# A two-layer decoder trunk: first projections by pairs of row blocks, cond fetched first, ada groups placed behind the compression, elementwise work moved from POOL to DVE and ACT

## The chip, the cores and the metric

The kernel runs on one core of a Trainium2 chip. The metric is the device time of one execution in microseconds (us). An execution that the hardware profiler recorded is read here by its engines: PE (matrix products and transposes), DVE (vector), ACT (activations), POOL (the second elementwise engine) and SP, whose queue issues nearly all weight loads.

## The reference

The reference is a trunk of two layers over 256 tokens of width 1024, all in float32. Each layer is a mixer and a mixture of experts, both behind a norm that is scaled and shifted by a vector made of the condition `c` ("ada"):

```python
cond = jax.nn.silu(c)
for layer in range(DEPTH):                      # DEPTH = 2
    mod = cond @ ada_w[layer] + ada_b[layer]    # 1024 x 6144
    sh1, sc1, g1, sh2, sc2, g2 = jnp.split(mod, 6, axis=-1)
    h = modulate(rms_norm(x, norm_mix[layer]), sh1, sc1)
    y = nsa_conv_mixer(h, ...) if layer % 2 == 0 else rwkv_pool_mixer(h, ...)
    x = x + g1[:, None, :] * y
    h = modulate(rms_norm(x, norm_ffn[layer]), sh2, sc2)
    x = x + g2[:, None, :] * grouped_moe(h, ...)   # 16 experts, top 2 of one group
return rms_norm(x, final_norm)
```

The mixer of layer 0 is sparse attention beside a gated convolution. Its attention has three branches: keys and values compressed by a small MLP with GELU, blocks selected by the compressed scores, and a window. The mixer of layer 1 is RWKV-7 (a recurrence over time with decay, here solved in chunks) beside causal means over windows of 2 to 16 tokens.

## The kernel before

Tokens lie in two blocks of 128 (`tt`), channels in eight row blocks of 128 (`kt` or `ct`). Weights come as pieces of 1 MB (128 x 2048 float32). `stream` takes the next slot of a ring of `NB` = 10 buffers and issues the load on SP's queue, so a load starts only when the last reader of its slot is through, and SP's queue is served in order. Engines run their instructions in the order that the program's scheduler fixed at build time. `tc.issue_after(d)` is a bound for that scheduler: what is inside comes behind the instruction `d`.

The work runs in stages, by the profiled execution: start and projections (0 to 61 us), compression (61 to 91), the attention loop (91 to 171), router and gather of layer 0 (`into_moe`, 171 to 207), its experts (`moe`, 207 to 413), the transition (413 to 429), the mixer of layer 1 (`mixer1`, 429 to about 587), its router (587 to 617), its experts (617 to 823) and the tail.

The ada vectors aren't made on PE. Weight pieces are laid out with the output on the partitions, and each piece takes two DVE instructions at L200 (`scalar_tensor_tensor` with a running sum, 128 x 1024), four for a group `ada(l, n)` of 512 outputs. Each layer has twelve groups, 48 of these instructions. Groups 0 to 3 are wanted by the first norm, 4 and 5 by the residual gate, 6 to 11 by the norm and gate of the experts. In layer 0, groups 0 to 3 stand in front of the projections (`TokProj`, L456 to L471, PE L471), 4 and 5 behind them, 6 and 7 in the compression, 8 behind it, and the list `more` in the attention loop (L720 to L735, ten steps `i`) names the others and three groups of layer 1. The fourth, (1, 3), is loaded in `moe` and computed in `start` (L1609).

The compression takes the GELU at L611 to L616 (tile `hg`), PE L625 and L630, the scores at L644 to L658 (`Pc`), and the transposes L664. `fill.run(n)` puts n units of the convolution's projections (PE L557, two row blocks each) into PE's order at such places, so that PE has work while DVE and ACT finish a chain. `heat(n)` issues n matrix products whose result nobody reads.

In layer 1, weights are split into a high part (ACT, L387) and a rest (L388, POOL or DVE by the list `engs` of `Parts`); a projection is three products per row block (PE L426). Behind it stands one long chain through DVE, ACT and POOL: shifts (L1198), key norms and gates (L1233 to L1271, POOL at L1246 and L1255), `AR` (POOL L1277), `rk` (DVE L1282), the chunk products (PE L1322, masks on DVE L1324 and L1326 and on POOL L1330 and L1332), `solve` (L1340, a triangular inverse of small DVE steps from PE L1345 on), `spread`, and the levels (PE L1374, DVE L1380 and L1386) that fold the chunks. The windowed means are `pooled` (POOL L1426, then PE L1440).

In the router, `choose` (L769) turns logits into a selection (L783 to L799), `place` (PE L808) into positions. `split` (L292) makes the high part and the rest of the normed tokens, the rest on ACT and POOL (L299, L300).

## Time and profile before

| | us |
|---|---|
| median of 3 executions | 836.95 (835.94 to 837.11) |
| the profiled execution's own time | 836.91 |
| its span, first to last instruction | 835.2 |
| PE busy in the span | 745.1 (89%) |
| DVE busy | 441.8 (53%) |
| ACT busy | 222.9 (27%) |
| POOL busy | 103.2 (12%) |
| moved by DMA | 291.34 MB, 349 GB/s in the mean |

A share of the whole span says little here, since the stages have different limits: the two expert stages, half of the span, keep PE busy nearly without a gap, and POOL does nothing in them. So the views are read stage by stage: the busy time of each engine in a stretch, what PE waited for, and which instructions of an engine are long where another runs beside them.

### The profile page before, as it was taken

To read this page: it belongs to the slowest core of one execution; us is meant where nothing else is said; L and a number is where in the kernel's file an instruction comes from. 1 tells how busy PE (TensorE), PEld (TensorE's weight loads), DVE (VectorE), ACT (ScalarE), POOL (GpSimd) and SP (SyncE) were. 2 spreads that over 40 slices of the span, in tenths; PEclk is the share of its full clock that TensorE was granted. 3 is DMA by queue.
4 is the path that set the end of the run, shared out by engine and by line. 5 is a ranking of instruction groups with operands and counts; after the bars stand their busy time and mean duration, and the time that the engine had idled before them with its cause. 6 is when DMAs were issued, how large, how long until landed. Compare 5 with 4: busy or idle time off the path is not lost.

```text
span 835.2 us, 12029 instructions
## 1 busy us (share of the span) xinstructions
PE 745.1 (89%) x4778; PEld 419.5 (50%) x4779; DVE 441.8 (53%) x937; ACT 222.9 (27%) x442; POOL 103.2 (12%) x87
## 2 busy tenths in 40 slices
PE   0998989996999999999669859799889999999993
PEld 0556766455353353533268859567553534435331
DVE  5666769954123342223788898986531421434225
ACT  3031313245111121201357633303531201202112
POOL 0000132511000000000223794100110000000000
PEclk9999989998999999999969988899979999999998
DMA  9999959897899999999856175787839999999991
GB/s 362 415 420 421 365 197 344 299 419 297 363 421 422 422 421 421 423 421 424 351 201 252 51 305 226 320 320 287 350 151 421 423 423 421 423 420 423 420 417 73
DMA packets 42689, 291.34 MB, mean 349 GB/s; under 512 B 4864, under 2 KB 5504, under 8 KB 8448
## 3 DMA queue, kind: packets, MB, share of 16 engines
q1 hardware_dynamic: 41760, 288.07, 85.1%
q10 hardware_dynamic: 864, 2.40, 0.8%
q8 instruction: 42, 0.69, 0.3%
q14 instruction: 23, 0.19, 0.1%
HBM read 289.40 MB, written 1.05 MB: 348 GB/s over the span
## 4 chain that ended last, share of the span: by engine, by line
PE 36%; DVE 7%; issue 3%; POOL 2%; ACT 2%; POOLq 0%; DVEq 0%; ACTq 0%
PE ps L985 13%; PE ps L1017 6%; PE ps L426 3%; PE ps L361 3%; PE ps L1374 3%; PE ps L1037 2%; PE ps L900 1%; DVE w L200 1%; DVE slab L1326 1%; POOL wr L388 1%; POOL AR L1277 1%; PE ps L1322 1%; POOL slab L1255 1%; PE ps L773 1%; DVE slab L140 0%
## 5 line engine op out<-in xcount | busy, mean ns | idle before, releaser
L985 PE MATMUL ps<-w,XT 128*64 128x512 f32 x1024 | 223.8, 595 | 0.0
L985 PEld LDWEIGHTS ps<-w,XT 128*64 128x64 f32 x1024 | 73.7, 138 | 146.3 <-issue 143.2
L200 DVE SCALAR_TENSOR_TENSOR w<-w,cond 128x1024 f32<-128x1024 f32 x96 | 120.0, 1279 | 11.5 <-ACT cond L148 6.3
L990 DVE TENSOR_TENSOR sg<-sg,ps 128x512 f32<-128x512 f32 x16 | 11.0, 687 | 199.5 <-PE ps L985 199.5
L1017 PE MATMUL ps<-w,HT 128*64 128x512 f32 x512 | 113.8, 596 | 1.3 <-ACT HT L1004 1.3
L1017 PEld LDWEIGHTS ps<-w,HT 128*64 128x64 f32 x512 | 35.2, 137 | 70.5 <-issue 63.0
L426 PE MATMUL ps<-hT,wr 128*128 128x256 f32 x288 | 56.5, 299 | 5.6 <-issue 4.1
L361 PE MATMUL ps<-w,slab 128*128 128x512 f32 x128 | 61.5, 619 | 0.0
L1022 DVE SCALAR_TENSOR_TENSOR Y<-ps,gw,Y 128x512 fp32r<-128x512 f32 x32 | 24.0, 750 | 63.0 <-ACT Y L1021 63.0
L388 POOL TENSOR_TENSOR wr<-w,wr 128x2048 fp32r<-128x2048 f32 x5 | 24.7, 4943 | 224.0 <-SPq L1079 211.5
L426 PEld LDWEIGHTS ps<-hT,wr 128*128 128x128 f32 x288 | 48.1, 205 | 6.7 <-issue 4.7
L1021 ACT ACTIVATE Y<-ps,gw 128x512 fp32r<-128x512 f32 x32 | 22.0, 687 | 98.2 <-PE ps L1017 98.2
L372 DVE TENSOR_TENSOR x<-x,ps 128x512 f32<-128x512 f32 x72 | 46.3, 679 | 0.3
L557 PE MATMUL ps<-hT,w 128*128 128x256 f32 x192 | 46.0, 397 | 0.0
L371 DVE TENSOR_TENSOR ps<-ps,gb 128x512 f32<-128x512 f32 x64 | 41.4, 692 | 2.6 <-PE ps L1037 2.4
L426 PE MATMUL ps<-lo,wr 128*128 128x256 f32 x144 | 42.5, 295 | 0.0
L1037 PE MATMUL ps<-Y,CT 128*128 128x512 f32 x128 | 39.1, 422 | 2.9 <-ACT Y L1021 1.7
L557 PEld LDWEIGHTS ps<-hT,w 128*128 128x128 f32 x192 | 37.2, 198 | 6.1 <-issue 0.8
L471 PE MATMUL ps<-w,hT 128*128 128x512 f32 (+1 forms) x96 | 36.6, 541 | 0.3 <-ACT hT L271 0.2
L989 ACT ACTIVATE sg<-ps 128x512 f32<-128x512 f32 x16 | 9.6, 597 | 99.2 <-PE ps L985 99.2
L361 PEld LDWEIGHTS ps<-w,slab 128*128 128x128 f32 x128 | 23.4, 195 | 23.4 <-issue 22.2
L271 ACT ACTIVATE XT<-ps,AB 128x256 f32<-128x256 f32 x32 | 18.1, 565 | 62.0 <-PE ps L900 50.8
(319 smaller groups left out, 945.3 us busy)
## 6 DMA issues: line engine op xcount, KB each, us to landing
w<-in_moe_g_dram SPq DMA_DIRECT2D x64, 1024.0 KB, 16.0
w<-in_moe_u_dram SPq DMA_DIRECT2D x64, 1024.0 KB, 14.9
w<-in_moe_d_dram SPq DMA_DIRECT2D x60, 1024.0 KB, 16.0
w<-in_ada_w_dram SPq DMA_DIRECT2D x48, 1024.0 KB, 10.0
w<-in_w_dram SPq DMA_DIRECT2D x19, 1024.0 KB, 11.8
w<-in_wout_dram SPq DMA_DIRECT2D x8, 1024.0 KB, 9.6
w<-in_cmp_w_dram SPq DMA_DIRECT2D x4, 1024.0 KB, 12.9
w<-in_moe_d_dram SPq DMA_DIRECT2D x4, 512.0 KB, 17.9
```

Source lines behind the costliest of these rows:

```text
L200: V.scalar_tensor_tensor(ws, ws, 1.0, cond, op0=OP.mult, op1=OP.mult, accum_out=modc[:, l, k:k + 1])
L361: mm(st[h], self.oT(kt)[:, tt * 128:(tt + 1) * 128], self.ws[h][kt // 4][:, (kt % 4) * 512:(kt % 4 + 1) * 512], start=kt == 4, stop=kt == 3)
L371: V.tensor_mul(po, po, gb[:, sl])
L372: V.tensor_add(x[:, tt, sl], x[:, tt, sl], po)
L388: eng.tensor_tensor(lo, raw, hi, op=OP.subtract)
L426: mm(pq, a, b, start=first and kt == kts[0] and i == 0, stop=last and kt == kts[-1] and i == 2)
L471: mm(self.pq[tt], hT[:, kt, tt * 128:(tt + 1) * 128], self.w[:, k * n:(k + 1) * n], start=kt == 0, stop=kt == 7)
L557: mm(st["pq"], w(kt, ct * 128, ct * 128 + 128), hT[:, kt, :], start=kt == 0, stop=kt == 7)
L985: mm(pg[64 * e:64 * e + 64, :], XT[:, kt, 64 * e:64 * e + 64], ws[kt // 4, e][:, (kt % 4) * 512:(kt % 4 + 1) * 512], start=kt == 0, stop=k ...
L1017: mm(py[64 * e:64 * e + 64, :], HT[:, c, 64 * e:64 * e + 64], ws[e][:, c * 512:(c + 1) * 512], start=c == 0, stop=c == 3)
L1037: mm(po, CT[:, tt], Y[:, i, h * 512:(h + 1) * 512], start=i == 0, stop=i == 1)
L1374: mm(t[x[o], p], left(p, *x), right(p, *x), start=start and p == 0, stop=stop and p == 3)
```

## The change

Nothing that is computed changes. The parts:

- **Ring.** `NB` is 12 for 10, with less scratch for DMA descriptors; in `moe` one buffer of the pool `wq` goes, and 20 pieces of the experts are loaded ahead instead of 19.
- **Start.** `cond` is the first load, in two halves on two queues; its SiLU stands behind the loads of the constants. The first projections go by pairs of row blocks (`pair`, `mod_pair`, `cols`): the ada pieces of one pair, then its products. The bias adds of the first four groups go to DVE.
- **Compression.** `ada(0, 4)` comes behind the last instruction of the GELU, 5 and 6 behind `vcm`, 7 behind `Pc`; `more` holds 8, 9, 10 and 11. Five fills of PE become seven, three become five.
- **Attention loop.** POOL's half of L690 goes to ACT.
- **Router.** The rest in `split` is one DVE instruction (128 x 1024) ahead of the scores; `heat(10)` in layer 0, `heat(4)` for `heat(2)` and the gather ahead of the gate units in layer 1. `ada(1, 3)` moves to the end of layer 0's router.
- **Transition.** The first piece of layer 1's projection is loaded and split inside the last expert step; the rest of it, `heat(16)` and `heat(4)` stand by the norm; both `ab` come first.
- **Mixer of layer 1.** All POOL work goes to DVE: the splits, L1246, L1255, L1277, masks L1330 and L1332, `pooled`. `rk` and the masks come behind `solve`, as do all ada pieces of groups 4 to 11. Copies of `tok_kb` and `tok_v` (half of them DVE L140) go to ACT. `spread` may come at 11 us of filling instead of 14.
- **Tail.** `x * fin` of one half is made early, and ACT scales it; the output is issued ahead of the branch for the overflow.

```diff
-NB = 10
+NB = 12
...
-    nc.scalar.dma_start(cond, bass.AP(tensor=ca.tensor, offset=ca.offset, ap=[[0, 128], [1, D]]))
-    P.activation(cond, cond, AF.Silu)
+    for eng, o in ((nc.sync, 0), (nc.scalar, 64)):
+        eng.dma_start(cond[o:o + 64], bass.AP(tensor=ca.tensor, offset=ca.offset, ap=[[0, 64], [1, D]]))
...
-                G.tensor_tensor(hl[:, 1, sl], t, hl[:, 0, sl], op=OP.subtract)
+            V.scalar_tensor_tensor(hl[:, 1], x[:, tt], r, hl[:, 0], op0=OP.mult, op1=OP.subtract)
...
+        nxt = norm.pair(0)
         for h in range(2):
-            ada(0, h)
-            ada(0, 2 + h)
-            norm.ab(h)
...
+            for q in (2 * h, 2 * h + 1):
+                for n in (h, 2 + h):
+                    cols(n, q % 2, 1 if q else 2)
+                norm.mod_pair(q, nxt)
+                for t in projs[:2]:
+                    if q % 2 == 0:
+                        t.load(h)
+                    t.run(q)
...
-        for n in (4, 5):
-            ada(0, n)
...
-        ada(0, 6)
+        with tc.issue_after(d.ins):
+            ada(0, 4)
         fill.add(chan_units(1304 + 1024, done_cg))
-        fill.run(5)
+        fill.run(7)
...
-        ada(0, 7)
+        with tc.issue_after(d.ins):
+            ada(0, 5)
+            ada(0, 6)
...
-        ada(0, 8)
-        fill.run(3)
+        with tc.issue_after(d.ins):
+            ada(0, 7)
+        fill.run(5)
...
-                    eng = V if hh else G
-                    eng.tensor_scalar(Pt[:, hh, b], Pt[:, hh, b], mx[:, 2 * hh + b, 2:3], None, op0=OP.mult)
+                    if hh:
+                        V.tensor_scalar(Pt[:, hh, b], Pt[:, hh, b], mx[:, 2 * hh + b, 2:3], None, op0=OP.mult)
+                    else:
+                        P.activation(Pt[:, hh, b], Pt[:, hh, b], AF.Copy, scale=mx[:, 2 * hh + b, 2:3])
...
-        more = [(0, 9), (0, 10), (0, 11), None, None, None, None, (1, 0), (1, 1), (1, 2)]
+        more = [(0, 8), (0, 9), (0, 10), None, (0, 11), None, None, (1, 0), (1, 1), (1, 2)]
...
+            heat(10)
             route.place(1)
+            ada(1, 3)
...
+                            gs_.append(Parts(1536, 256, ((None, None),), (V,)).split(lo=False))
+                            first.extend((gs_[0].last, gs_[0].finish(0)))
...
-        gs_.append(Parts(0, 512, (("B6", None), (None, None)), (G, V)))
+        gs_.append(Parts(0, 512, (("B6", None), (None, None)), (V, V)))
...
-        G.tensor_tensor(av, av, kk, op=OP.mult)
+        V.tensor_tensor(av, av, kk, op=OP.mult)
...
-                G.tensor_tensor(SC[c][own, h, :, 0], SC[c][own, h, :, 0], K("scmask")[own, None, 0:64].to_broadcast([64, 4, 64]), op=OP.mult)
...
+        late = deque([weigh] + [lambda c=c: masks(c) for c in range(4)])
...
-                for _ in range(4):
-                    todo.popleft()(last)
+                solved.append(last)
...
-            if steps == 1 and spent >= 14:
+            if steps == 1 and spent >= 11:
...
-        norm.ab(0)
-        for tt in range(2):
-            d = norm.transposes(tt, 0)
-        for h, t in enumerate(todo):
-            with tc.issue_after(d[1] if h else last):
-                ada(1, 3, [t], h)
-        norm.ab(1)
+        for h in range(2):
+            norm.ab(h)
...
-    nc = _bacc.Bacc("TRN2", target_bir_lowering=False, num_devices=1)
+    nc = _bacc.Bacc("TRN2", target_bir_lowering=False, num_devices=1, dynamic_dma_scratch_size=64)
```

The scheduler's order shows where this lands. First DVE's order at the end of the compression, where `m` is the softmax's denominators of the two token blocks, `slab` from `s` is `Pc`, and the instruction on `w, modc` is an ada instruction (L200 before, L201 after). Before:

```order
L655 TENSOR_TENSOR m_546<-m_546,gs 128x8
L655 TENSOR_TENSOR m_568<-m_568,gs 128x8
L657 TENSOR_SCALAR m_546<-m_546,c_m_169 128x8
L658 TENSOR_TENSOR slab_102<-s_567,m_568 128x8x16
L200 SCALAR_TENSOR_TENSOR w,modc<-w,cond 128x1024 x2
L658 TENSOR_TENSOR slab_102<-s_545,m_546 128x8x16
L200 SCALAR_TENSOR_TENSOR w,modc<-w,cond 128x1024 x2
L140 COPY PcT<-ps 128x256
```
After, from the middle of the same chain:

```order
L201 SCALAR_TENSOR_TENSOR w,modc<-w,cond 128x1024 x2
L699 TENSOR_SCALAR m_550<-m_550,c_m_202 128x8
L695 TENSOR_REDUCE m_572<-s_571 128x8
L700 TENSOR_TENSOR slab_103<-s_549,m_550 128x8x16
L696 RECIPROCAL m_572<-m_572 128x8
L606 TENSOR_SCALAR slab_104<-slab_100,vec 128x256
L201 SCALAR_TENSOR_TENSOR w,modc<-w,cond 128x1024 x2
L697 TENSOR_TENSOR m_572<-m_572,gs 128x8
L607 SCALAR_TENSOR_TENSOR slab_104<-slab_100,vec,slab_104 128x254
L700 TENSOR_TENSOR slab_103<-s_571,m_572 128x8x16
L608 SCALAR_TENSOR_TENSOR slab_104<-slab_100,vec,slab_104 128x255
L201 SCALAR_TENSOR_TENSOR w,modc<-w,cond 128x1024 x2
```
The ada pairs, which stood behind `Pc` of a block, stand inside the chain of both blocks, among the filters of the convolution (L606 to L608).

DVE's order in the transition, from the scaling of `x` by the norm (`w` from `x, rms`) to the high and low parts of the transposed tokens (`hT`, `lo`). Before:

```order
L1065 TENSOR_SCALAR w<-x,rms 128x1024
L1079 UNCONDITIONAL_BRANCH x2
L200 SCALAR_TENSOR_TENSOR w,modc<-w,cond 128x1024
L269 TENSOR_SCALAR ps<-ps,AB 128x128 x4
L289 TENSOR_TENSOR lo<-ps,hT 128x2x128 x4
L200 SCALAR_TENSOR_TENSOR w,modc<-w,cond 128x1024 x2
L263 SCALAR_TENSOR_TENSOR AB<-modc,vec 128x4
L269 TENSOR_SCALAR ps<-ps,AB 128x128 x4
```
After:

```order
L1117 TENSOR_SCALAR w<-x,rms 128x1024
L1139 UNCONDITIONAL_BRANCH x2
L270 TENSOR_SCALAR ps<-ps,AB 128x128 x5
L306 TENSOR_TENSOR lo<-ps,hT 128x2x128 x2
L270 TENSOR_SCALAR ps<-ps,AB 128x128
L306 TENSOR_TENSOR lo<-ps,hT 128x2x128 x2
L436 TENSOR_TENSOR wr<-w,wr 128x1024
L306 TENSOR_TENSOR lo_2850<-ps,hT 128x2x128 x2
```
The ada instructions of (1, 3) are gone from among the modulated transposes, and half of a weight split (L436) stands there.

DVE's order ahead of the first level (`Wm` from `ps`), where `pool` is the windowed means. Before:

```order
L200 SCALAR_TENSOR_TENSOR w,modc<-w,cond 128x1024
L1438 TENSOR_TENSOR pool<-pool,slab_3297 128x16
L200 SCALAR_TENSOR_TENSOR w,modc<-w,cond 128x1024 x9
L263 SCALAR_TENSOR_TENSOR AB<-modc,vec 128x4
L264 COPY AB<-modc 128x4
L263 SCALAR_TENSOR_TENSOR AB<-modc,vec 128x4
L756 TENSOR_TENSOR r_ab<-rw,AB 128x128
L200 SCALAR_TENSOR_TENSOR w,modc<-w,cond 128x1024 x2
L1380 TENSOR_TENSOR Wm<-ps,c_m_2882 128x256 x2
```
After:

```order
L201 SCALAR_TENSOR_TENSOR w,modc<-w,cond 128x1024
L1502 TENSOR_TENSOR pool<-pool,slab_3329 128x16
L201 SCALAR_TENSOR_TENSOR w,modc<-w,cond 128x1024 x11
L264 SCALAR_TENSOR_TENSOR AB<-modc,vec 128x4
L201 SCALAR_TENSOR_TENSOR w,modc<-w,cond 128x1024
L1444 TENSOR_TENSOR Wm<-ps,c_m_2910 128x256 x2
L201 SCALAR_TENSOR_TENSOR w,modc<-w,cond 128x1024
L1444 TENSOR_TENSOR Wm<-ps,c_m_2910 128x256 x2
```
In both, ada instructions stand in a run in front of the first level: 12 in the rows of before, 13 in those of after, and four more a few rows ahead of these. Counted from the end of layer 0, 28 stood ahead of that place, and now 21.

## Rows read from the trace of the kernel before

**Rows 1.** Windows: stretch, length; PE, PEld, DVE, ACT, POOL busy; PEclk, DMA share, GB/s.

```profile
91.40:171.00 79.60, 73.82 (x392) 49.39 (x392) 64.90 (x159) 20.30 (x81) 24.49 (x24) 0.94 0.78 294
206.60:412.70 206.10, 203.98 (x1013) 85.22 (x1012) 65.30 (x115) 36.30 (x58) 0.00 (x0) 1.00 0.99 411
412.70:428.70 16.00, 3.68 (x18) 3.33 (x17) 14.89 (x22) 8.01 (x15) 9.81 (x2) 0.66 0.57 201
428.70:477.30 48.60, 48.40 (x362) 45.37 (x362) 40.37 (x59) 35.31 (x55) 19.61 (x8) 0.94 0.42 166
477.30:530.50 53.20, 38.47 (x609) 35.43 (x609) 49.64 (x95) 17.53 (x36) 32.73 (x26) 0.87 0.70 275
530.50:616.70 86.20, 78.68 (x892) 55.04 (x892) 60.07 (x162) 30.30 (x61) 7.86 (x9) 0.90 0.76 289
```

**Rows 2.** Waits of PE, whole span: releaser, us in total, times, longest.

```profile
PE ps L280 <- DMA c_all<-in_c_all_dram: 21.1, 1, 21.1
PE ps L280 <- DVEq L1079: 8.3, 1, 8.3
PE ps L808 <- DVE r_sel L799: 7.3, 2, 5.1
...
PE ps L1440 <- DVE pool L1437: 4.7, 1, 4.7
...
PE ps L596 <- DVE slab L539: 1.9, 1, 1.9
...
PE ps L664 <- DVE slab L658: 1.7, 1, 1.7
```

**Rows 3.** Timeline of the transition: start, length, instruction, idle before and releaser.

```profile
414.68 2.63 DVE L1191 TENSOR_SCALAR om<-vec 128x14 f32<-128x14 f32 x1
...
419.82 5.30 POOL L388 TENSOR_TENSOR wr<-w,wr 128x2048 fp32r<-128x2048 f32 x1 [2.54 <-ACTq L1079]
...
421.02 5.19 DVE L200 SCALAR_TENSOR_TENSOR w<-w,cond 128x1024 f32<-128x1024 f32 x1 [0.26 <-DVEq L1079]
...
426.13 0.73 DVE L269 TENSOR_SCALAR ps<-ps,AB 128x128 f32<-128x128 f32 x2
```

**Rows 4.** Groups of DVE, 412 to 531: count, busy us, mean ns, idle before.

```profile
L200 DVE SCALAR_TENSOR_TENSOR w<-w,cond 128x1024 f32<-128x1024 f32 x16 | 24.5, 1567 | 0.3 <-DVEq L1079 0.3
L388 DVE TENSOR_TENSOR wr<-w,wr 128x2048 fp32r<-128x2048 f32 x4 | 14.7, 3670 | 4.3 <-ACT wr L387 4.3
L1282 DVE SCALAR_TENSOR_TENSOR slab<-slab,vec,slab 128x256 f32<-128x256 f32 x4 | 7.3, 1892 | 0.0
L1326 DVE TENSOR_TENSOR slab<-slab,c_m 64x256 f32<-64x256 f32 x8 | 6.6, 819 | 0.2
L1198 DVE SCALAR_TENSOR_TENSOR slab<-ps,vec,slab 128x255 f32<-128x255 f32 x12 | 5.4, 475 | 2.1 <-ACT slab L1197 1.9
L140 DVE COPY slab<-ps 64x512 f32<-64x512 f32 x6 | 4.1, 689 | 0.2
```

**Rows 5.** The same view of POOL, 412 to 531.

```profile
L388 POOL TENSOR_TENSOR wr<-w,wr 128x2048 fp32r<-128x2048 f32 x5 | 24.7, 4943 | 224.0 <-SPq L1079 211.5 <-ACT wr L387 9.9 <-ACTq L1079 2.5
L1330 POOL TENSOR_TENSOR slab<-slab,c_m 64x256 f32<-64x256 f32 x8 | 11.4, 1426 | 0.3
```

**Rows 6.** Timeline of DVE: one split with POOL idle.

```profile
437.14 2.29 DVE L388 TENSOR_TENSOR wr<-w,wr 128x2048 fp32r<-128x2048 f32 x1 [0.87 <-ACT wr L387]
```

**Rows 7.** Source line L1326: least, median and longest ns of its eight.

```profile
L1326 DVE TENSOR_TENSOR slab<-slab,c_m x8: 418/828/1279, 488.3 to 496.9; 64x256 f32<-64x256 f32 x8
```

**Rows 8.** Groups of DVE in the attention loop, 91.4 to 171.

```profile
L200 DVE SCALAR_TENSOR_TENSOR w<-w,cond 128x1024 f32<-128x1024 f32 x30 | 36.0, 1229 | 0.0
```

**Rows 9.** Timeline of DVE in the router of layer 1, beside POOL.

```profile
610.07 1.18 DVE L797 SCALAR_TENSOR_TENSOR r_tm<-r_bi,r_v,r_tm 128x16 f32<-128x16 f32 x1
```

**Rows 10.** Timeline of the tail: the second half of the final norm.

```profile
828.95 1.28 DVE L1067 SCALAR_TENSOR_TENSOR w<-x,rms,cond 128x1024 f32<-128x1024 f32 x1
```

**Rows 11.** DMA issues of the page: count, KB, median us to landing.

```profile
w<-in_ada_w_dram SPq DMA_DIRECT2D x48, 1024.0 KB, 10.0
```

More of the change, by code (lines that the diff above doesn't have):

```diff
@@ L1164, in mixer1 @@
         gs_[1].load()
-        with tc.issue_after(d[0]), tc.issue_after(d[1]):
-            gs_[1].split()
-        gs_.append(Parts(0, 512, (("B6", None), (None, None)), (G, V)))
+        for i in range(2):
+            with tc.issue_after(d[0]), tc.issue_after(d[1]):
+                gs_[1].split(i + 1)
+        gs_.append(Parts(0, 512, (("B6", None), (None, None)), (V, V)))
         def vc(o, ct):
@@ L1509, in mixer1 @@
         for i in range(4):
-            fill.add(units(gs_[4], i, shifted(8, lambda i: vR[:, i])))
+            fill.add(units(gs_[4], i, shifted(8, lambda i: vR[:, i], lambda: solved)))
         fill.run(9.28)
@@ L1539, in mixer1 @@
             u()
+            with tc.issue_after(solved[0]):
+                if late:
+                    late.popleft()()
         step(fill.all())
@@ L1608, in trunk, with start @@
     state, fin = [], []
-    def start(pool, l, rms, xs, todo, last):
+    def start(pool, l, rms, xs, w):
         norm = Norm(l, 0, rms, xs, pool)
-        preload(AF.Sigmoid, xs[:, 1, 0:1])
-        norm.ab(0)
-        for tt in range(2):
-            d = norm.transposes(tt, 0)
-        for h, t in enumerate(todo):
-            with tc.issue_after(d[1] if h else last):
-                ada(1, 3, [t], h)
-        norm.ab(1)
-        for tt in range(2):
-            d = norm.transposes(tt, 1)
+        for h in range(2):
+            norm.ab(h)
+        for h in range(2):
+            for tt in range(2):
+                d = norm.transposes(tt, h)
+            if h == 0:
+                with tc.issue_after(d[1]):
+                    w.finish(1)
+        heat(4)
         return norm, d
```

182 lines of the change are left out of this document (114 added, 68 removed).

## The prediction

> **What bounds the kernel now.** I read the windows first, to see which engine is full in which stage [rows 1]. In the expert stage PE works 203.98 of 206.10 us, and POOL not at all: what is late at its start is late at its end, and the change moves its inside little. From the end of layer 0's experts to 530.5 us it is another picture. PE is busy 3.68 + 48.40 + 38.47 = 90.55 of 117.80 us there, DVE 14.89 + 40.37 + 49.64 = 104.90. DVE is the bound of that stretch, with 12.90 us idle, and beside it POOL is busy 9.81 + 19.61 + 32.73 = 62.15 us. Second, PE's waits [rows 2]: the long ones behind the start (8.3 us in the transition, 7.3 at the router's positions, 4.7 at the windowed means) all end with DVE. Third, why DVE is full. Its groups hold instructions that are far too long for their size [rows 4]: an ada instruction of 128 x 1024 takes 1567 ns in the mean, in the attention loop 1229 [rows 8]; a weight split takes 3670, with POOL idle 2.29 us [rows 6]; L1326 takes between 418 and 1279 ns for one and the same form [rows 7]. The timeline shows the cause at its plainest: an ada instruction that began at 421.02, 1.2 us behind a split on POOL, took 5.19 us, and the modulation of the transposes, queued behind it, ran at 426.13 [rows 3].
>
> So the question is what becomes of DVE when POOL's 62 us come over to it.
>
> **Mixer of layer 1 and transition.** First what goes, against a price from undisturbed rows. Ada: 24.5 - 16 x 1.23 = 4.8 us. Splits: 14.7 - 4 x 2.29 = 5.5. L1282: 7.3 for four, where the shift of nearly the same size has 475 ns: 5.4. L1326: 6.6 - 8 x 0.42 = 3.2. L1191, 14 columns, 2.63 us: by the same 475 ns it loses 2.2. Together 21.1 us of excess [rows 3, 4, 6 to 8].
>
> Then what comes. Of POOL's 62.15 us, the splits are 24.7 in five, on DVE 5 x 2.29 = 11.5. For the other 37.4 the rows give two ratios: 2.29 to 4.943 (0.46), and for the masks 0.42 to 1.426 (0.29) [rows 5 to 7]. That is 11.0 to 17.3, in all 22.5 to 28.8; I take the middle, 25.7, since the rest are instructions of both kinds.
>
> What leaves DVE: six copies to ACT, 4.1 us [rows 4], which ACT has room for (17.53 busy of 53.20, rows 1). And by the order of both kernels seven ada instructions fewer stand between layer 0 and the first level (21 for 28): 7 x 1.23 = 8.6. Net: -21.1 + 25.7 - 4.1 - 8.6 = **-8.1 us** of DVE's work.
>
> The idle 12.90 us are waits for ACT's casts (4.3 in front of splits, rows 4), for POOL in the chain, and for PE. Moving `rk` and the masks behind `solve` and having two more slots in the ring shortens some, and the copies make others; nothing in the trace prices it. Bounds are 0 and all of it; I take half, 6.5. The first level then begins 14.6 us earlier. The ends: 8.1 - 3.1 (the dear price) = 5.0 earlier, and 8.1 + 3.2 + 12.9 = 24.2 earlier. PE sets a limit of its own, 117.80 - 90.55 = 27.3. The transition is in this sum: its 8.3 us wait holds L1191, and its 5.19 us ada instruction is gone from there. [...]
>
> Levels to router: three of the seven ada instructions come back among the levels, 3.7 us on a DVE that is busy 60.07 of 86.20 there [rows 1]; a third on the path, **+1.2**.
>
> [...]
>
> **Layer 0's mixer.** Start: PE's first transposes wait 21.1 us for the constants [rows 2]. The first pair needs about 5.7 MB (four ada pieces, `cond`, `x`, constants), 13.9 us at the 411 GB/s that the loads reach when saturated [rows 1]; so 0 to -7.2, taken -4. The early ada groups no longer stand ahead of the compression, so the 1.9 us wait of L596 goes. But the order shows six ada instructions inside the chain that ends in `Pc`, where two stood: 4 x 1.23 = +4.9 on top of the 1.7 us wait of L664 [rows 2, 8]; two more fill units ahead of it only move work. Entry into the loop: -1.0. In the loop, DVE is busy 64.90 of 79.60 us, and its ada instructions crowd into the last four steps: 28 stand there, of the 30 of before [rows 8] six lay earlier, so 24. Four more are +4.9 us on the side that ends last. Against it POOL's share of L690 is off, the fills are three units shorter (PE has 73.82 us of work there), and the router has its selection beside an idle POOL: together perhaps -4. Sum **0**, with ends at -6 and +6.
>
> **Router of layer 1 and tail.** An instruction on 16 columns took 1.18 us beside POOL [rows 9], at 475 ns or less it and its neighbour give back about 1.2; the gather ahead of the gate units fills part of the 7.3 us wait of L808: **-2.2**. The tail scales one half on ACT instead of two on DVE of 1.28 us in a row [rows 10]: **-1**.
>
> **Sum.** 0 - 14.6 + 1.2 - 2.2 - 1 = -16.6 us. The profiled execution took 836.91 us (its span 835.2 and 1.7 around it), and the median is 836.95, so the two are one: **820 us**.
>
> **The rivals.** (1) *The excess is DVE's own.* If long instructions are long for another reason (operands that come late), the 21.1 us stay, DVE gets POOL's work on top, and the end is 820.3 + 21.1 = 841 us, slower than before. It decides as soon as 16.6 of the 21.1 stay. For it: the trace shows no stage where DVE does this work with POOL empty. Against: the split at 2.29 and the loop's 1229 ns [rows 6, 8]. 7 in 100.
> (2) *PE becomes the bound.* DVE's idle time goes, the cheap price holds: -24.2 for -14.6, so 811 us, 807 at PE's limit. For it: the solve now stands ahead of work that nobody waits for. 18 in 100.
> (3) *Ada instructions wait for their pieces ahead of the levels.* Seventeen stand there on nine pieces; some of these pieces can only be loaded when an earlier one of the same run has left its slot. A load takes 10.0 us in the median [rows 11], the six instructions between cover 6 x 1.23 = 7.4, so three turns cost 3 x 2.6 = 7.8 and everything behind them on DVE, the level's products first, waits: 828 us. The rows show that DVE does not overtake: the modulation waited out the 5.19 us [rows 3]. Against it, the median is made in saturated stages, and here the DMA share is 0.42 to 0.76 [rows 1]. 14 in 100.
> [...]
> (4) *The attention loop loses.* The four added ada instructions stay on the path and nothing of the -4 comes: 824 to 826 us. 14 in 100.
> (5) *The parts don't act:* pieces come no earlier, waits change their names, 837 us. 5 in 100.
>
> **How the numbers follow.** The forecast has 42 in 100, 814 to 824 us. Leaving out (1) and (5) and a little at either end, the range is 804 to 833 us. Faster by over 0.2% (about what a measurement of this kernel can tell from no change) is the forecast with (2), (3) and (4): 0.88. Within it is (5): 0.05. Slower is (1): 0.07.
>
> **What would show it.** Right: in the changed profile POOL is nearly idle, L388's successor on DVE takes 2.3 us each time, the masks 0.42, ada instructions 1.23 all through the mixer of layer 1, and the first level begins about 15 us earlier, counted from the end of layer 0's experts; those begin within 6 us of 206.6, and each expert stage is as long as before. Wrong: DVE instructions that stay long with POOL idle (1); PE without gaps from the transition to the levels (2); DVE waiting for ada pieces (3); a later start of the experts of layer 0 (4). I would be wrong beyond the range if the two expert stages changed in length, since half of the time lies there and I left them as they are.

## The result, and the profile after

The changed kernel takes **823.74 us** (median of four runs, 822.52 to 826.12), the kernel before 837.03 (four runs, 835.94 to 837.46): ratio 0.9847, interval 0.9820 to 0.9873. A second set beside other kernels gave 823.26 (822.81 to 824.34) against 836.83, ratio 0.9844 (0.9825 to 0.9862). The forecast was 820 with a range of 804 to 833: the sign and the range hold, and the time lies at the upper edge of the likeliest case (814 to 824). The profiled execution took 824.72 us, its span 822.9.

The stages of the two profiles, from the first instruction of each (us; "level" is DVE's first evacuation into `Wm`, "solve" the first instruction on `xd`):

| | before | after | difference of the length |
|---|---|---|---|
| start to layer 0's experts | 206.63 | 208.89 | **+2.3** (forecast 0) |
| layer 0's experts | 412.32 | 416.24 | **+1.7** (forecast 0) |
| transition, to the first projection | 428.67 | 426.57 | -6.0 |
| projections, to the products | 477.28 | 477.55 | +2.4 |
| products, to the solve | 502.25 | 490.60 | -11.9 |
| solve and fills, to the first level | 549.16 | 538.71 | +1.2; last four **-14.4** (forecast -14.6) |
| levels, to the router | 587.23 | 577.95 | **+1.2** (forecast +1.2) |
| router, to layer 1's experts | 616.68 | 605.54 | **-1.9** (forecast -2.2) |
| layer 1's experts and tail | 835.16 | 822.88 | **-1.1** (forecast -1) |

So in this execution the terms of layer 1 came out nearly as summed, and all that is missing lies in layer 0, where I had put two zeros. How much of that split belongs to this one execution is taken up at the end.

The windows of the changed kernel (stretch, length; PE, PEld, DVE, ACT, POOL busy; PEclk, DMA share, GB/s), answering [rows 1]: the attention loop, layer 0's experts, the transition, the projections, the products, solve and fills, and the way from the experts to the first level as one.

```profile
94.20:173.00 78.80, 70.32 (x373) 45.62 (x373) 67.39 (x164) 26.33 (x96) 1.90 (x9) 0.90 0.76 295
208.90:416.20 207.30, 205.23 (x1012) 85.44 (x1012) 65.86 (x115) 36.27 (x57) 0.00 (x0) 0.99 0.96 403
416.20:426.60 10.40, 6.73 (x39) 3.61 (x38) 7.55 (x20) 6.94 (x18) 0.00 (x0) 1.00 0.43 130
426.60:477.50 50.90, 46.52 (x359) 42.83 (x359) 45.07 (x62) 36.20 (x54) 0.20 (x1) 1.00 0.61 235
477.50:490.60 13.10, 13.05 (x239) 12.42 (x239) 7.65 (x19) 7.19 (x17) 0.00 (x0) 0.87 0.98 388
490.60:538.70 48.10, 40.47 (x491) 30.32 (x491) 45.75 (x119) 16.77 (x33) 3.82 (x4) 0.89 0.66 252
...
416.20:538.70 122.50, 106.78 (x1124) 89.18 (x1125) 106.02 (x218) 67.09 (x121) 4.02 (x5) 0.94 0.66 249
```

The same stretch of the kernel before, for the sum below, and its products:

```profile
412.30:549.20 136.90, 109.12 (x1106) 94.20 (x1106) 121.00 (x212) 64.63 (x115) 64.59 (x38) 0.86 0.60 231
...
477.30:502.30 25.00, 14.46 (x239) 13.00 (x240) 24.50 (x31) 7.66 (x18) 23.30 (x15) 0.81 0.69 264
```

POOL fell from 64.59 us to 4.02 there. The products, where DVE had been busy 24.50 of 25.00 us, are now PE's: 13.05 of 13.10. The groups of DVE from the experts to the first level (count, busy us, mean ns, idle before) answer [rows 4, 6, 7]:

```profile
L201 DVE SCALAR_TENSOR_TENSOR w<-w,cond 128x1024 f32<-128x1024 f32 x21 | 24.7, 1215 | 0.0
L402 DVE TENSOR_TENSOR wr<-w,wr 128x2048 fp32r<-128x2048 f32 x8 | 18.1, 2286 | 1.4 <-ACT wr L400 1.4
...
L1387 DVE TENSOR_TENSOR slab<-slab,c_m 64x256 f32<-64x256 f32 x8 | 3.4, 420 | 0.2
...
L1588 DVE SCALAR_TENSOR_TENSOR slab<-slab,vec,slab 128x256 f32<-128x256 f32 x4 | 1.7, 477 | 0.0
```

Splits 2.29 us each time, masks 0.42, ada instructions 1.215, the bonus weights (L1282 before, L1588 now) 0.477 instead of 1.892: what the prediction named as its sign. PE's waits over the whole span (releaser, us in total, times, longest) answer [rows 2]:

```profile
PE ps L282 <- DVE xn L275: 17.2, 2, 16.8
PE ps L1504 <- DVE pool L1501: 7.6, 1, 7.6
PE ps L853 <- DVE r_sel L844: 6.0, 2, 3.8
PE ps L745 <- ACT slab L735: 4.9, 1, 4.9
...
PE ps L707 <- DVE slab L700: 2.9, 1, 2.9
...
PE ps L297 <- DVEq L1139: 2.3, 1, 2.3
...
PE ps L707 <- DVE m L696: 1.8, 1, 1.8
```

The 21.1 us at the start are 17.2, the 8.3 us of the transition are 2.3 (L297), the wait for the windowed means (L1440 before) has grown from 4.7 to 7.6, the 1.7 us at the transposes of `Pc` (L664 before) are 2.9 and 1.8 (L707), and one is new: 4.9 us in the attention loop behind the scaling of `Pt` that the change gave to ACT.

### The profile page after: what moved, and what is told of

Same layout as the page of the kernel before. It is cut to its first block, busy times and chain, and to the rows that moved or that the text cites. A ratio compares the mean times of both kernels' runs of the same rounds, so it can differ in the third digit from the quotient of the medians.

```text
span 822.9 us, 12042 instructions
## 1 busy us (share of the span) xinstructions
PE 747.0 (91%) x4810; PEld 414.7 (50%) x4811; DVE 432.0 (52%) x975; ACT 227.6 (28%) x453; POOL 9.5 (1%) x28
## 5 line engine op out<-in xcount | busy, mean ns | idle before, releaser
L1063 PE MATMUL ps<-w,HT 128*64 128x512 f32 x512 | 115.5, 603 | 1.4 <-ACT HT L1050 1.4
L201 DVE SCALAR_TENSOR_TENSOR w<-w,cond 128x1024 f32<-128x1024 f32 x80 | 94.7, 1215 | 0.0
L374 PE MATMUL ps<-w,slab 128*128 128x512 f32 x128 | 59.7, 604 | 0.0
L448 PE MATMUL ps<-hT,wr 128*128 128x256 f32 x288 | 52.2, 283 | 3.3 <-ACT hT L304 2.5
L448 PEld LDWEIGHTS ps<-hT,wr 128*128 128x128 f32 x288 | 44.1, 188 | 4.7 <-ACT hT L304 3.2
L596 PE MATMUL ps<-hT,w 128*128 128x256 f32 x192 | 45.4, 394 | 0.0
L448 PE MATMUL ps<-lo,wr 128*128 128x256 f32 x144 | 40.5, 281 | 0.1
L596 PEld LDWEIGHTS ps<-hT,w 128*128 128x128 f32 x192 | 37.2, 197 | 5.8 <-issue 0.5
L494 PE MATMUL ps<-w,hT 128*128 128x512 f32 (+1 forms) x96 | 38.5, 560 | 0.7 <-ACT hT L272 0.7
L946 PEld LDWEIGHTS ps<-Pp,hl 128*128 128x128 f32 x224 | 28.7, 198 | 5.3 <-issue 5.3
## 6 DMA issues: line engine op xcount, KB each, us to landing
w<-in_cmp_w_dram SPq DMA_DIRECT2D x4, 1024.0 KB, 12.9
```

The costliest lines, as they stand in the source:

```text
L201: V.scalar_tensor_tensor(ws, ws, 1.0, cond, op0=OP.mult, op1=OP.mult, accum_out=modc[:, l, k:k + 1])
L374: mm(st[h], self.oT(kt)[:, tt * 128:(tt + 1) * 128], self.ws[h][kt // 4][:, (kt % 4) * 512:(kt % 4 + 1) * 512], start=kt == 4, stop=kt == 3)
L448: mm(pq, a, b, start=first and kt == kts[0] and i == 0, stop=last and kt == kts[-1] and i == 2)
L494: mm(self.pq[tt], hT[:, kt, tt * 128:(tt + 1) * 128], self.w[:, k * n:(k + 1) * n], start=kt == 0, stop=kt == 7)
L596: mm(st["pq"], w(kt, ct * 128, ct * 128 + 128), hT[:, kt, :], start=kt == 0, stop=kt == 7)
L946: mm(pgs[ct // 2][:, ct % 2], norm.parts[tt][:, i, ct * 128:(ct + 1) * 128], Pp[:, tt].rearrange("p e s -> p (e s)"), start=start and i == ...
```

## The experiments

Marks of all profiles, in us (begin of layer 0's experts, their end, first projection of layer 1, products, solve, first level, begin of layer 1's experts, end). The marks come from one execution of each kernel, the medians from four to ten.

| run | experts 0 | end 0 | proj. | prod. | solve | level | experts 1 | end | median |
|---|---|---|---|---|---|---|---|---|---|
| before | 206.63 | 412.32 | 428.67 | 477.28 | 502.25 | 549.16 | 616.68 | 835.16 | 837.03 |
| after | 208.89 | 416.24 | 426.57 | 477.55 | 490.60 | 538.71 | 605.54 | 822.88 | 823.74 |
| e1 pool back | 209.77 | 415.37 | 425.69 | 479.64 | 502.49 | 545.77 | 612.67 | 830.00 | 829.10 |
| e2 only dve | 206.71 | 412.47 | 429.69 | 476.69 | 496.87 | 545.33 | 613.48 | 831.93 | 832.49 |
| e3 fills back | 206.45 | 412.32 | 423.40 | 474.40 | 486.89 | 536.60 | 603.87 | 821.18 | 820.86 |
| e4 ada back | 203.02 | 410.40 | 420.78 | 471.76 | 484.82 | 532.92 | 598.54 | 815.86 | 818.40 |
| e5 first back | 205.36 | 411.44 | 422.47 | 473.44 | 485.92 | 535.65 | 602.97 | 820.42 | 822.23 |
| e6 late first | 206.46 | 413.85 | 426.99 | 476.91 | 489.40 | 539.25 | 606.90 | 824.29 | 825.77 |
| e7 pieces late | 207.49 | 414.87 | 425.19 | 476.16 | 489.19 | 533.58 | 606.14 | 823.44 | 826.04 |
| e8 both | 200.51 | 406.45 | 417.53 | 468.50 | 480.98 | 527.04 | 599.68 | 817.00 | 822.67 |
| e9 again | 206.55 | 413.88 | 424.20 | 475.19 | 488.25 | 536.34 | 603.60 | 820.97 | 823.26 |
| e10 ada again | 200.38 | 406.18 | 417.33 | 468.31 | 480.80 | 530.43 | 599.42 | 816.75 | 818.60 |
| e11 l690 | 207.28 | 413.73 | 424.24 | 475.23 | 488.28 | 536.69 | 604.03 | 821.33 | 820.03 |
| e12 no heat | 207.39 | 414.66 | 425.88 | 476.87 | 489.92 | 538.95 | 606.22 | 823.56 | 825.51 |

### Is it POOL, or the order? (e1, e2)

**e1** is the changed kernel with POOL's work of layer 1 given back, in the new order:

```
-  gs_.append(Parts(0, 512, (("B6", None), (None, None)), (V, V)))
+  gs_.append(Parts(0, 512, (("B6", None), (None, None)), (G, V)))
   ... and so one split each of three more weights, av, csx, the AR products,
   the masks and the windowed sums: V -> G
```

> The changed kernel with the elementwise work of the mixer of layer 1 given back to POOL (one of two splits of each pair, both products with kk and sg, AR, all masks, the windowed means); every order bound and placement of the change stays, and its copies on ACT. Theory A, as predicted: the gain from the transition to the levels is DVE freed from POOL, whose instructions stretch DVE's own. Then most of it goes: 831 to 838 us, ada instructions beside POOL above 1.4 us, masks on DVE above 0.7 us in the mean, splits on DVE above 3 us. Rival B: the gain is the order (ada instructions, masks and rk out of the chain, the early first piece), and who does the elementwise work matters little: 821 to 827 us. If the time comes out between, it is shared, and the first level's start against the end of layer 0's experts (122.3 us in the changed kernel, 136.7 before) says by how much.

**e2** is the kernel before with the same work moved to DVE and nothing else (the mirror of that diff, V for G).

> The kernel before with one thing changed: the same elementwise work of layer 1's mixer, the split of the first piece included, on DVE instead of POOL. No order bound moves. Theory A's own sum for this: DVE loses 21.1 us of excess and takes 25.7 us, so it is no less full than before, and only the waits for POOL in the chain go (2.3 in front of the second key product, 3.1 of PE for AR); 831 to 838 us, so the move alone gives little and needs the order. Rival C: the move alone is the gain, 823 to 828 us. Rival D, the excess is DVE's own: 21 us of work are added without return, 850 us or more.

e1: 829.10 us (827.45 to 835.34, ten runs), ratio 0.9924 (0.9897 to 0.9950). e2: 832.49 (830.46 to 834.39, ten runs), ratio 0.9954 (0.9934 to 0.9973). From the end of layer 0's experts to the first level it is 136.8 us before, 132.9 with the move alone, 130.4 with the order alone, and 122.5 with both: -4.0 and -6.4 apart, -14.4 together. With the other half in place, the move is worth 7.9 and the order 10.4. e1's order isn't wholly that of the changed kernel: the scheduler put 16 ada instructions ahead of the first level there, for 21 in the changed kernel, so its stretch holds some 6 us less of DVE's work (5 x 1.215). The rival that the long instructions are DVE's own falls: in e2, in the old order, they shrink at once. Its window and groups of DVE:

```profile
412.50:545.30 132.80, 103.58 (x1104) 89.30 (x1104) 118.33 (x238) 64.60 (x115) 3.56 (x7) 0.87 0.60 234
```

```profile
L200 DVE SCALAR_TENSOR_TENSOR w<-w,cond 128x1024 f32<-128x1024 f32 x28 | 32.8, 1219 | 0.3 <-DVEq L1079 0.3
L388 DVE TENSOR_TENSOR wr<-w,wr 128x2048 fp32r<-128x2048 f32 x9 | 20.3, 2285 | 2.5 <-ACTq L1079 1.6 <-ACT wr L387 0.9
...
L1330 DVE TENSOR_TENSOR slab<-slab,c_m 64x256 f32<-64x256 f32 x8 | 3.3, 416 | 0.1
...
L1240 DVE SCALAR_TENSOR_TENSOR slab<-slab,vec 128x256 f32<-128x256 f32 x4 | 1.7, 480 | 0.0
```

With POOL back (e1) they are long again, in the new order:

```profile
L402 DVE TENSOR_TENSOR wr<-w,wr 128x2048 fp32r<-128x2048 f32 x4 | 16.3, 4069 | 9.2 <-ACT wr L400 9.2
L1387 DVE TENSOR_TENSOR slab<-slab,c_m 64x256 f32<-64x256 f32 x8 | 10.3, 1285 | 0.2
...
L1329 DVE TENSOR_TENSOR dec<-slab,gm 128x12 f32<-128x12 f32 x1 | 2.4, 2382 | 0.0
```

But e1's ada instructions stay at 1214 ns, where theory A wanted over 1400, and e1 is faster than A's 831: it lies between the two. Which of its instructions ran beside POOL, and which of two such instructions was the long one, is said further below. e2 lies in A's 831 to 838.

### The transition (e6, e12)

**e6** loads and splits the first projection's weights after the last expert pass, as before, whole and on DVE; ada group 3 stays in the router.

```
-  gs_.append(Parts(1536, 256, ((None, None),), (V,)).split(lo=False))   # inside the last pass
+  gs_.append(Parts(1536, 256, ((None, None),), (V,)).split())           # behind it
-  w.finish(1)                                                           # in start
```

> The changed kernel with the first projection piece of layer 1 loaded and split where the kernel before has it, behind the last expert pass, whole and on DVE; the ada pieces of group 3, which the change moves into the router, stay moved. It asks which of the two shortened the transition from 16.35 to 10.33 us. E, the early piece did: the transition takes 13.5 to 16 us and the whole 827 to 830 us. G, the ada instructions that left did: the transition stays at 10 to 11.5 us and the whole within 1.5 us of 823.7.

825.77 us (824.72 to 826.13), ratio 0.9875 (0.9846 to 0.9904). The transition takes 13.14 us, between the two expectations: of the 6.0 us gained, the early piece has 2.8, and the rest of the change there 3.2 (ada group 3 off DVE, the split off POOL, the filler; no run parts these). In e6's profile the clock fell for 3.41 us in the transition (granted 0.87 in the mean of its window), in that of the changed kernel it did not (1.00). The profiles that have the early piece and such a fall (e3, e5, e8, e10, below) take 11.0 to 11.2 us there, so by them the early piece has 2.0 to 2.1.

**e12** is the changed kernel without `heat(16)` and `heat(4)`.

> The changed kernel without its two runs of filler matmuls between the last expert pass and the first projection of layer 1. The prediction counted them at nothing and the clock of that stretch at nothing. N, that is right: the transition and the projections take 10.3 and 51.0 us as with them, 823 to 825 us in all. [...]

825.51 us (824.46 to 827.01), 2.2 more than the changed kernel on the same chip (e9, 823.26). The whole lies above N's 823 to 825, and of N's two stages only the transition is longer. The windows of e12:

```profile
414.70:425.90 11.20, 4.02 (x19) 3.29 (x17) 7.47 (x20) 6.92 (x17) 0.00 (x0) 0.54 0.46 142
425.90:476.90 51.00, 47.89 (x363) 44.32 (x364) 45.17 (x62) 36.22 (x54) 0.20 (x1) 0.97 0.60 231
```

The transition runs at a granted clock of 0.54 in the mean instead of 1.00, and takes 0.9 us longer. The projections take 51.0 us as with the filler, although PE's busy time there is 1.4 higher (47.89 for 46.52, at a granted clock of 0.97 for 1.00): they have gaps that hide it (3.11 us for 4.38). But the filler does not always hold the clock. In the profiles of e3, e5, e8 and e10, which have it, the clock fell for 3.41 us over the transposes of the transition, and the stage took 11.0 to 11.2 us, as long as in e12 (e10's window):

```profile
406.20:417.30 11.10, 8.31 (x38) 5.17 (x36) 7.44 (x20) 6.87 (x17) 0.00 (x0) 0.85 0.49 149
```

So the filler was worth 0.9 us in the execution where the clock held (the profile of the result), and nothing in these. The rest of the 2.2 is not placed (in the profiles 0.8 of it lies in layer 0, which is the same code, and 0.9 between the solve and the first level).

### Layer 0 (e3, e4, e5, e9, e10, e11)

**e3** takes the added fill units out of the compression: `fill.run(7)` to 5 and `fill.run(5)` to 3. The argument of `fill.run` is not a number of units but a time in us, of which the kernel counts 1.73 for a unit (8 matrix products in the trace). So these are three units: ahead of the products on `hg` PE has 56 filling products in the changed kernel and 40 in e3 and before, from there to the transposes of `Pc` 32 and 24.

> The changed kernel with the fills of the compression as before (five and three units where the change has seven and five); the ada groups stay where the change puts them. [...] Theory M: the loop's end is set by DVE, on which 28 ada instructions stand in the last four steps; the fills then only move PE's wait from one place to another: start at 208 to 211 us, total 822 to 826 us.

**e4**, and once more **e10**, have in addition ada groups 4 to 11 where the kernel before has them:

```
+  for n in (4, 5):  ada(0, n)                # ahead of the compression
-  with tc.issue_after(d.ins): ada(0, 4)      # behind hg, vcm and Pc: 4 to 7
+  ada(0, 6)                                  # ... 6, 7, 8 there
-  more = [(0, 8), (0, 9), (0, 10), None, (0, 11), None, None, (1, 0), (1, 1), (1, 2)]
+  more = [(0, 9), (0, 10), (0, 11), None, None, None, None, (1, 0), (1, 1), (1, 2)]
```

> The changed kernel with the ada groups 4 to 11 of layer 0 and the fills as before (4 and 5 behind the projections, 6 and 7 in the compression, 8 behind it, 9 to 11 and three groups of layer 1 in the loop); the projections by pairs stay. Theory M: the ada groups behind the compression cost the loop more than they give the compression; with them back, the wait ahead of the compression's first product returns (1.9 us), the loop starts about 89 us and ends 3 to 5 us earlier, layer 0's experts start at 203 to 206 us, total 818 to 821 us. [...] Rival: the early groups eat what the pairs gave, since DMA is saturated until 100 us either way: 208 to 211 us, total 822 to 826 us.

> Ada back once more, with more rounds and beside the changed kernel on one chip, since its four times lay between 815.6 and 823.0 us. If the ada order and the fill units of layer 0 are worth something, it is 3 to 6 us faster than the changed kernel, 817 to 821 us, with the experts of layer 0 beginning at 200 to 204 us; if the first time was luck, the two are within 1.5 us of each other.

**e9** is the changed kernel once more, to see how far its layer 0 scatters.

> The changed kernel itself once more, beside the three that follow. Four profiles of the same code in layer 0's mixer (the changed kernel, pool back, late first, pieces late) have the experts of layer 0 begin at 208.89, 209.77, 206.46 and 207.49 us, against 206.63 and 206.71 with the old code (before, only DVE). R, the mixer is late by about 1.5 us in the mean, and the profile of the result happened to lie high: begin between 206.4 and 209.8 us, 822 to 825 us in all. P, the 2.3 us are exact: 208.5 to 209.3.

e3: 820.86 us (818.50 to 823.03), ratio 0.9804 (0.9770 to 0.9838). e4: 818.40 (815.62 to 822.98), 0.9794 (0.9744 to 0.9844). e10: **818.60 (816.64 to 821.35), ratio 0.9786 (0.9762 to 0.9811)**, 4.7 us less than e9 on the same chip. This version beats both kernels. e3's time lies below the 822 to 826 that M gave it, and its experts begin at 206.45, ahead of M's 208 to 211; e4's time is in the 818 to 821 that M gave that run. So the fill units and the ada order both count. e9: R holds; six profiles of the same new code in layer 0 (after, e1, e6, e7, e9, e12) have the experts begin at 206.46 to 209.77, in the mean 207.76, and two of the old code at 206.63 and 206.71. So the mixer's loss is about 1.1 us in the mean, with a scatter of 3.3 between the six, and the profile of the result lies high with its 2.3.

Where the ada order acts is seen in two stretches, from the products on `hg` to the transposes of `Pc` and from there to the router (windows of e3, of e10, of the kernel before, and the first of e9):

```profile
74.60:83.00 8.40, 8.40 (x84) 7.31 (x84) 6.08 (x24) 2.37 (x5) 0.20 (x1) 1.00 1.02 427
83.00:170.50 87.50, 76.27 (x398) 51.15 (x397) 74.58 (x182) 26.91 (x98) 2.10 (x10) 0.92 0.79 318
```

```profile
79.50:89.80 10.30, 8.57 (x83) 7.20 (x84) 6.36 (x25) 2.65 (x5) 0.00 (x0) 1.00 1.01 425
89.80:164.00 74.20, 69.98 (x398) 47.33 (x397) 66.53 (x163) 26.42 (x97) 2.55 (x8) 1.00 0.90 356
```

```profile
80.80:91.20 10.40, 8.63 (x84) 7.30 (x84) 6.42 (x25) 2.65 (x5) 0.00 (x1) 1.00 1.02 421
91.20:171.70 80.50, 74.72 (x397) 49.78 (x396) 65.10 (x159) 20.42 (x81) 24.49 (x24) 0.94 0.78 295
```

```profile
78.10:93.40 15.30, 10.62 (x92) 8.82 (x92) 11.39 (x36) 2.65 (x5) 0.20 (x1) 0.91 1.01 427
```

The first three have the same fill units, so they can be compared directly. With the new ada order (e3) the first stretch begins 4.9 us earlier than in e10 and is itself 1.9 shorter, with PE full for 8.40 of 8.40 us. Then the loop pays it back: 87.50 us for 74.20, with DVE busy 8.05 us more (41 ada instructions in it for 34) and idle 12.9 for 7.7. That is a loss of 6.5 us at the loop's end.

But e3's order on DVE is not that of the changed kernel, although only fill units differ in the source: without them the scheduler put two ada instructions between the products on `hg` and the transposes of `Pc` and the others behind `Pc`. In the changed kernel seven stand there (three in the kernel before), the stretch takes 15.3 us as in e9 (10.4 before, with one fill unit less), and PE waits 2.9 and 1.8 us at the transposes. So e3 changes two things, the fill units and the order.

In the loop of the changed kernel the place is plain; its timeline (start, length, instruction, idle before and releaser) in the fifth step:

```profile
137.34 1.21 DVE L201 SCALAR_TENSOR_TENSOR w<-w,cond 128x1024 f32<-128x1024 f32 x1
...
139.62 0.15 DVE L728 TENSOR_TENSOR mx<-mx,gs 128x4 f32<-128x4 f32 x1
...
139.88 0.91 ACT L735 ACTIVATE slab<-slab,mx 128x256 f32<-128x256 f32 x2 [4.10 <-DVE mx L728]
...
140.44 0.90 PE L745 MATMUL ps<-c_all,slab 128*128 128x128 f32 x3 [4.90 <-ACT slab L735]
```

Two ada instructions stand on DVE between the reciprocal of the row sums (136.67) and a product on 4 columns (139.62); ACT waits 4.10 us for that product and PE 4.90 for ACT. In e3 this wait of PE is gone, and PE waits 9.2 us in five pieces for copies on DVE (L140) instead, for 3.5 in e10.

**e5** is e4 with the first projections by halves again (`ada`, `ab`, `transposes` and `run(2 * h, 2 * h + 1)` for each half); `cond` still comes first.

> The changed kernel with two parts of layer 0's mixer as they were: the ada groups 4 to 11 and the fill units where the kernel before has them (as in the run ada back, 818.4 us, experts of layer 0 at 203.02 us), and in addition the first projections by halves instead of pairs of row blocks. cond is still fetched first on two queues. S, the pairs are worth the 4 us that the prediction gave the start: the experts of layer 0 begin at 206 to 207.5 us and the whole takes 821 to 823 us. N, the start is hidden later anyway (the gain of ada back came from the ada order alone): the experts begin at 202.5 to 204 us, 818 to 819.5 us.

822.23 us (821.05 to 822.78), ratio 0.9834 (0.9804 to 0.9864): S in the time. The experts begin at 205.36, against 201.30 in the mean of the three profiles with that ada order (e4 203.02, e8 200.51, e10 200.38): the pairs are worth 4.1 us by the profiles, 3.6 to 3.8 by the medians of e4 and e10.

**e11** is e4 with the first half of `Pt` scaled on POOL, as in the kernel before.

```
-  V.tensor_scalar(...) if hh else P.activation(..., AF.Copy, scale=...)
+  (V if hh else G).tensor_scalar(...)
```

> Ada back with one instruction form of the attention loop as before: the scaling of Pt's first half on POOL, not on ACT. The prediction counted its leaving POOL among the reliefs that give back 4 us in the loop. L, POOL's 4 instructions of a step slow DVE down as they did before: the loop (from the last transposes of Pc to the router) takes 2 to 4 us longer than with ada back, 820 to 823 us. Z, ACT was what the loop waited for (4.90 us once in the changed kernel): it takes as long or up to 2 us less, 816 to 819 us.

820.03 us (818.50 to 823.98), ratio 0.9809 (0.9782 to 0.9836), at L's lower edge, 1.4 above e10 with intervals that overlap. In its profile, an execution of 823.17, the loop takes 79.3 us against 74.2 in e10. So POOL's half costs something, between 1.4 us by the medians and 5 by the profiles; the size stays open.

### Ada ahead of the levels (e7, e8)

**e7** takes out the four ada instructions that stand between the bonus and the windowed means; they are read between the levels. In the order that the scheduler made of it nine move: 12 stand ahead of the first level, for 21 in the changed kernel.

```
-  todo[0](solved[0])
-  todo.popleft()
-      if len(todo) > 8:
-          todo.popleft()(solved[0])
```

> The changed kernel without the four ada instructions that it puts on DVE ahead of the second half of the windowed means and the first level (they began at 512.95, 515.55, 518.15 and 520.19 us); their pieces are read with the other ada work between the levels. [...] D, these four stand on the path: up to 4 x 1.15 = 4.6 us earlier at the first level, 818 to 821 us in all. W, they only move: the levels get longer by as much, 822.5 to 825 us.

**e8** is e7's edit and e4's together.

> The ada order and the fill units of layer 0's mixer as in ada back (818.4 us) together with the four ada instructions of layer 1 taken from ahead of the first level as in pieces late. If both are worth what they were supposed to be and touch different stages, 814 to 817 us: faster than the kernel before and than the changed one. If the four only move, 818 to 820 us.

e7: 826.04 us (825.04 to 827.49), ratio 0.9887 (0.9856 to 0.9918), worse than either theory; e8: 822.67 (818.86 to 823.36), 0.9842 (0.9817 to 0.9868), 4 us above e10 and above both of its expectations. The waits of PE in layer 1's mixer in e7, and the window of the levels in e7 and in the changed kernel:

```profile
PE ps L1504 <- DVE pool L1501: 4.2, 1, 4.2
PE ps L1438 <- DVE slab L140: 3.3, 1, 3.3
```

```profile
533.60:577.90 44.30, 38.65 (x666) 27.78 (x663) 39.92 (x89) 9.48 (x23) 1.92 (x5) 0.96 0.89 341
```

```profile
538.70:578.00 39.30, 37.48 (x669) 26.65 (x664) 30.30 (x74) 9.49 (x23) 0.72 (x3) 1.00 0.92 355
```

From the first projection to the first level e7 is 3.7 us shorter (108.4 for 112.1), and the levels are 5.0 longer, where DVE has 9.6 us more to do. So the 7.6 us wait for the windowed means was cover for ada work, not a loss that could be had back, and the place that the change chose is the better one.

## Why the prediction was right, and where it was not

**The transition and the mixer of layer 1 (-14.6, measured -14.4 in this profile): right in the sum, wrong in its halves.** I had DVE's work fall by 8.1 us and its idle time by 6.5. The windows say 121.00 to 106.02, that is -15.0, and idle 15.9 to 16.5. Two parts can be told apart by e2. Copies and seven ada instructions fewer were -12.7; from e2 to the changed kernel it is 118.33 to 106.02, -12.3. The move itself was -21.1 + 25.7 = +4.6, and e2 shows -2.7. The split of 2.29 us, POOL's other work (about 13.6 us by e2's groups, for 14.2 taken) and the excess of L1282, L1326 and the splits were as priced; L1240, 3.8 us for its four before and 1.7 in e2, was overlooked (-2.1), the ada excess was 5.7 (38.5 to 32.8 us for all 28) for 4.8, and the remaining 3 or so are spread over small groups, which these views don't resolve. The idle time that I halved did not shrink, it moved: in the projections it fell from 8.2 to 5.8 us and between the solve and the first level from 6.1 to 2.4, but in the products, where DVE was full and now waits for PE, it rose from 0.5 to 5.5, and in the transition from 1.1 to 2.9. That the two errors cancel is luck.

**"Ada instructions are long" was a mean that hid two.** [rows 4] give 1567 ns for sixteen. The one line that lists least, median and longest of all 28 up to the first level in the kernel before says what they are:

```profile
L200 DVE SCALAR_TENSOR_TENSOR w<-w,cond x28: 1201/1214/5186, 419.5 to 545.0; 128x1024 f32<-128x1024 f32 x28
```

Nearly all ran at 1.21; the excess is in the one of 5.19 us [rows 3] and one of 2.90 at 516.28. The price per instruction was right as a sum and wrong as a picture, and it is why e1, where by the two timelines only one of 16 ran beside POOL, has none of it (1214 ns in the mean).

**Layer 0's mixer (0, measured +1.1): a sum that met by chance.** In the means of the six profiles of the changed code and the two of the old, the loop begins 2.4 us later (last transposes of `Pc` at 93.7 for 91.3; forecast -1.0), takes 2.2 less (78.3 for 80.6; forecast +0.9), and the router of layer 0 takes 0.9 more (35.7 for 34.9; forecast: a part of the -4). The products on `hg` come 2.5 earlier, where -5.9 was forecast (-4 for the start, -1.9 for L596): "two more fill units ahead of it only move work" left their 3.5 us (2 x 1.73) out of the entry, and the same units' going was booked as a gain in the loop. Without the units, in e3, these products come 6.3 earlier (74.60). The step on the chain of `Pc` is right in size: +4.9 was summed, and from these products to the last transposes it is 15.3 us for 10.35. A third fill unit lies in it (1.7 us), so PE's wait there grew by only 3.0, from 1.7 to 4.7.

What a single edit is worth, the runs bound and don't fix. The pairs have 4.1 (e5; -4 taken). The ada order costs 5.1 by the profiles (206.45 in e3 for 201.30), 2.3 to 2.5 by the medians (some of them of different chips); the fill units 1.3 by the profiles (207.76 for 206.45), 2.4 to 2.9 by the medians. e3's profile is the slowest of its four executions (823.03, median 820.86), and e8's, one of the three behind the 201.30, the fastest of its five (818.86, median 822.67), so the 5.1 is likely high. The reliefs that I put at -4 are -1.3 in the net (201.30 + 4.1 = 205.4 for 206.67), and the router is 0.6 to 1.5 longer in the profiles, a term that I had left out. Ada group 3 is not its cause: in e4 and e10 it is the full 1.5, and no ada instruction stands in it.

**Layer 0's experts (0, measured +1.7): a clock that I had not counted.** The granted clock was 1.00 over the whole expert stage before. In the profile of the result it falls once, to 0.50, at 226.11 for 3.41 us; the windows of the changed kernel and of the one before round the same instructions (24 short ones for the routes, then the down projection):

```profile
222.80:226.10 3.30, 2.62 (x24) 2.21 (x24) 1.91 (x7) 1.17 (x2) 0.00 (x0) 1.00 1.02 429
226.10:229.50 3.40, 3.40 (x10) 0.98 (x8) 0.00 (x0) 0.00 (x0) 0.00 (x0) 0.50 1.00 417
```

```profile
220.50:223.80 3.30, 2.63 (x24) 2.20 (x24) 1.91 (x7) 1.17 (x2) 0.00 (x0) 1.00 1.01 425
223.80:227.20 3.40, 3.40 (x18) 1.15 (x16) 0.00 (x0) 0.00 (x0) 0.00 (x0) 1.00 1.03 429
```

The same busy times ahead of it, then 10 matmuls instead of 18. Six of the fourteen profiles have it (after, e4, e6, e7, e9, e12), and there the stage takes 207.3 to 207.4 us; in the other eight it takes 205.6 to 206.5. What decides it is not settled; it goes neither with an edit of that stage, of which there is none, nor with a median. Nor is it all lost: from the begin of layer 0's experts to the first level, the seven profiles with the same code there (after, e3, e4, e5, e9, e10, e11) take 329.4 to 330.3 us, for 342.5 before, that is -12.2 to -13.1. Where the fall comes in the experts, the stretch behind them takes 122.5 us; where it doesn't, 123.0 to 124.3, with a fall of 3.41 us in the transition. So the +1.7 and the -14.4 of the result belong together: for the two stages as one, -14.6 was forecast and about -12.6 measured, and that the second came out so close alone is luck.

**The rest.** Levels +1.2 (+1.2), router of layer 1 -1.9 (-2.2), tail -1.1 (-1). With +1.1 and +1.7 in layer 0 the sum is 820.3 + 2.8 = 823.1, within 0.7 of either median.

**The rivals.** (1), excess of DVE's own, fell with e2. That all of the 21.1 us would go once POOL is empty was an estimate that nothing showed before the result; in e2, in the old order and with POOL busy for 3.56 us, the splits took 2.285 us in the mean, L1326 0.420, L1282 0.473 and the ada instructions 1.219. (2), PE as the bound, holds in the products alone. (3), pieces that come too late ahead of the levels, came to nearly nothing: in the profile of the result thirteen ada instructions run from 522.32 to 537.45 without a gap, and DVE then waits 1.25 us for PE. Waits of DVE for a piece there are short in the others too: 0.77 us in e9, 0.70 in e12, 1.94 in e7 and 1.96 in e8, for 7.8 forecast. (4), the loop, came in its sign and not in its place: the experts of layer 0 begin 1.1 us later in the mean and its 824 to 826 us are just above the result, but the loop itself is 2.2 us shorter than before. The 4.9 us wait above is what it loses against e10, whose loop takes 74.2.

## What to carry to other kernels

Moving work off a second engine and reordering for it were worth 4 and 6.4 us alone and 14.4 together: measure both halves before dropping either. Work that is pushed out of a chain lands somewhere; before counting it as free, look which engine ends last in the place where it lands (here DVE, in the attention loop), and whether filler that covers that place was moved away. Where a scheduler fixes the order, taking one thing out moves others: e1, e3 and e7 moved ada instructions that their edits don't name, so count them in the trace before you give a difference to the edit. Of a group with a large mean, read the least, the median and the longest before pricing each of its instructions.
